# A hybrid Gated-DeltaNet and window-attention layer: the value head moved forward, inverses held back, small copies on ScalarE, two projections once over their weights

## The chip, the cores and the metric

One core of one Trainium2 chip. The metric is the device time of one execution in microseconds; the kernel before was run three times for it. TensorE does the matrix products, VectorE, ScalarE and GpSimd the rest; the profile names these engines PE (with PEld for its weight loads), DVE, ACT and POOL, and SP is the queue that issues most transfers.

## The reference, cut to what matters

The input is x of 2048 tokens by 1024 channels, float32. One projection w_in gives the inputs of two token mixers; their outputs are gated, merged, projected by w_out, added to the residual and normalized.

```python
q, k, v = split(silu(causal_conv4(h[..., :1536])))
o_a = chunked_gated_delta_rule(l2norm(q) * 128**-0.5, l2norm(k), v, g, beta)
y_a = o_a * rsqrt(mean(o_a**2) + 1e-6) * dn_norm_w * silu(dn_z)
q_b, k_b = partial_rope(sw_q), partial_rope(sw_k)
y_b = banded_sink_attention(q_b, k_b, v_b, sinks) * silu(sw_z)
merged = sigmoid(gate_a) * (y_a @ w_branch[0]) + sigmoid(gate_b) * (y_b @ w_branch[1])
out = merged @ w_out
r = alpha * x + out
y = (r - mean(r)) * rsqrt(var(r) + 1e-5) * ln_g + ln_b
```

The delta rule (four heads of 128) goes over blocks of tokens: a triangular system per block is inverted, and a state S of 128x128 per head is carried from block to block. The window attention has eight query heads of 64 in two groups of four, each with one key head, and looks back 128 tokens.

## The kernel before

**Tiling.** The tokens go in four chunks of T = 512, each of NB = 4 blocks of 128. Every product is float32 in three fast products: both factors are split into a high and a low part, and high x high, high x low and low x high are summed in PSUM (`prods`, L175 to L177). The split weights are made in chunk 0, kept in DRAM, and fetched again for each use in later chunks (tile wb, four buffers, `W_SPLIT`; the DRAM tensors are named kw_ and the weight, kw_o for the output projection).

**The order of TensorE's work** is written by hand. `ORDER` (L45) is a string of pieces for chunks 1 to 3 (`ORDER_FIRST`, L44, for chunk 0): kv, key and value rows of the window; k0 to k3, q0 to q3, v0 to v3, the projections of a head of the delta rule, each with its convolution (`conv_silu`, L309: a copy xs, three steps L318 and the end L321 on VectorE, with a halo of three columns carried from chunk to chunk); p, a quarter of the output projection of the chunk before (`project`, L674); g and z, gates; w0 and w1, the query projections of the window with rope (`window_q`, L541). After the fourth p the layer norm of the chunk before is spawned (`layer_norm`, L703; its rows are L718 and L719).

The class `Order` (L821) interleaves these dense pieces with tasks that have to wait for other engines: after each dense step it advances a planned time and lets a task make its next step if the latency written beside it (the `LAT_` numbers, L40) has passed. `finish(name)` runs the tasks up to that one with no dense work between: it moves the planned time on. The tasks of a head are `front` (decays, L365 for k, L389 for the triangular system), `inverse` (L423: the tile su is fetched by a transfer, a part of it zeroed at L924, and 16 steps L936 and L937 on VectorE solve the diagonal blocks of 32), `levels` (L428 to L472, the larger blocks), L485 (v transposed on TensorE), and `back`, the recurrence over the four blocks: L497 (S times k), bt L499 on VectorE, L502 and L505 on TensorE, wc L504 on VectorE, L508 and L510 on TensorE, S L509 on VectorE. `query_rows` (L560) transposes the roped queries (L565) and `attend` (L574) does the window attention.

**Query projection before.** `window_q` makes two passes, of two token blocks each. The first pass fetches four quarters of the weights and keeps them, the second uses the kept ones. Behind each pass come the ropes of its two blocks (`rope`, L877: a copy kr on ScalarE at L881, four small operations on VectorE at L885 to L887) and a task for their transposes. The second pass is followed by `st.finish("qT0")`. `project` makes two passes over kept quarters in the same way, and adds x at L688 (yBh, yBl).

The order on the other engines follows from a scheduler; each engine executes its list in order. The functions with the line numbers of the profile:

## Time and profile before

| | us |
|---|---|
| median of 3 runs | 1702.67 (1699.82 to 1708.82) |
| profiled execution | 1703.38 |
| its span, first to last instruction | 1701.6 |
| TensorE busy | 1623.3 (95%) |
| VectorE busy | 1019.1 (60%) |
| ScalarE busy | 534.6 (31%) |
| GpSimd busy | 313.1 (18%) |

The span is what the profile shows of the execution; the rest of the execution's time lies around it. The mean granted clock of TensorE is 0.987 of full speed. Matrix products are pipelined, so the busy time of TensorE is not its time at peak. A wait is put down to what came last.

### The profile page before, as it was taken

To read this page: it belongs to the slowest core of one execution; us is meant where nothing else is said; L and a number is where in the kernel's file an instruction comes from. 1 tells how busy PE (TensorE), PEld (TensorE's weight loads), DVE (VectorE), ACT (ScalarE), POOL (GpSimd) and SP (SyncE) were. 2 spreads that over 40 slices of the span, in tenths; PEclk is the share of its full clock that TensorE was granted. 3 is DMA by queue.
4 is the path that set the end of the run, shared out by engine and by line. 5 is a ranking of instruction groups with operands and counts; after the bars stand their busy time and mean duration, and the time that the engine had idled before them with its cause. 6 is when DMAs were issued, how large, how long until landed. Compare 5 with 4: busy or idle time off the path is not lost.

```text
span 1701.6 us, 27308 instructions
## 1 busy us (share of the span) xinstructions
PE 1623.3 (95%) x9846; PEld 1365.4 (80%) x9846; DVE 1019.1 (60%) x3202; ACT 534.6 (31%) x1484; POOL 313.1 (18%) x318
## 2 busy tenths in 40 slices
PE   8989999989979999999999999999999999999997
PEld 6867878878968778788987877888887887888787
DVE  6687678447577756434548774733556777463155
ACT  3454445424222432331302343323120244232110
POOL 4543544441401111010101111001010111100001
PEclk9999999999999999999999999999999999999999
DMA  8765676657765446457566644646566654564762
GB/s 304 237 228 186 200 256 200 232 194 251 249 240 177 141 127 177 141 161 238 170 213 208 184 138 129 192 137 199 170 195 212 201 159 119 149 190 143 272 207 77
DMA packets 189159, 323.39 MB, mean 190 GB/s; under 512 B 31072, under 2 KB 45408, under 8 KB 188896
## 3 DMA queue, kind: packets, MB, share of 16 engines
q1 hardware_dynamic: 185184, 316.40, 58.5%
q0 software_dynamic: 3840, 5.25, 1.5%
q8 instruction: 78, 1.28, 0.3%
q14 instruction: 57, 0.47, 0.1%
HBM read 244.97 MB, written 71.37 MB: 186 GB/s over the span
## 4 chain that ended last, share of the span: by engine, by line
PE 80%; DVE 9%; DMA 7%; ACT 1%; issue 1%; SPq 1%; POOL 1%; ACTq 0%; DVEq 0%; POOLq 0%
PE mm L175 22%; PE mm L177 21%; PE mm L176 21%; DMA wb<-kw_o 2%; PE pp L630 2%; PE pp L622 2%; DVE xt L936 1%; PE pp L591 1%; DVE xi L937 1%; PE pd L508 1%; PE pp L592 1%; PE pd L502 1%; DMA s<-in_lnp 1%; DVE k L318 1%; PE pd L510 1%
## 5 line engine op out<-in xcount | busy, mean ns | idle before, releaser
L175 PE MATMUL mm<-xh,wb 128*128 128x512 f32 x1128 | 472.0, 418 | 3.1 <-DVE mv L692 1.6
L177 PE MATMUL mm<-xh,wb 128*128 128x512 f32 x1128 | 447.4, 397 | 0.0
L176 PE MATMUL mm<-xl,wb 128*128 128x512 f32 x1128 | 445.8, 395 | 0.0
L177 PEld LDWEIGHTS mm<-xh,wb 128*128 128x128 f32 x1128 | 213.1, 189 | 50.3
L175 PEld LDWEIGHTS mm<-xh,wb 128*128 128x128 f32 x1128 | 214.1, 190 | 47.2 <-issue 4.5
L176 PEld LDWEIGHTS mm<-xl,wb 128*128 128x128 f32 x1128 | 215.0, 191 | 37.4
L157 POOL TENSOR_TENSOR wb<-w,wb 128x512 fp32r<-128x512 f32 (+1 forms) x110 | 146.3, 1332 | 182.2 <-ACT wb L156 167.8
L175 PE MATMUL mm<-wb,s 128*128 128x256 f32 x384 | 111.8, 291 | 10.3 <-DMA wb<-kw_o 6.3
L175 PE MATMUL mm<-wb,xh 128*128 128x256 f32 (+1 forms) x384 | 114.0, 297 | 6.6 <-DVE ba L264 3.2
L176 PE MATMUL mm<-wb,xh 128*128 128x256 f32 (+1 forms) x384 | 108.5, 282 | 0.3 <-POOL wb L157 0.3
L176 PE MATMUL mm<-wb,s 128*128 128x256 f32 x384 | 108.5, 283 | 0.0
L177 PE MATMUL mm<-wb,s 128*128 128x256 f32 x384 | 108.5, 283 | 0.0
L177 PE MATMUL mm<-wb,xl 128*128 128x256 f32 (+1 forms) x384 | 108.1, 281 | 0.0
L156 ACT ACTIVATE wb<-w 128x512 fp32r<-128x512 f32 (+1 forms) x110 | 68.9, 628 | 106.9 <-PE mm L177 54.6
L936 DVE TENSOR_TENSOR xt<-su,xi 128x16 f32<-128x16 f32 (+15 forms) x256 | 88.4, 345 | 5.7
L175 PEld LDWEIGHTS mm<-wb,s 128*128 128x128 f32 x384 | 73.1, 190 | 14.6 <-DMA wb<-kw_o 8.2
L608 ACT ACTIVATE s<-s,nm 128x256 f32<-128x256 f32 (+1 forms) x128 | 62.6, 491 | 68.4 <-DVE nm L602 68.4
L175 PEld LDWEIGHTS mm<-wb,xh 128*128 128x128 f32 x384 | 72.5, 189 | 10.0 <-issue 6.2
L937 DVE TENSOR_REDUCE xi<-xt 128x8 f32<-128x16 f32 (+15 forms) x256 | 74.7, 292 | 6.2
L176 PEld LDWEIGHTS mm<-wb,s 128*128 128x128 f32 x384 | 73.1, 190 | 0.2
L177 PEld LDWEIGHTS mm<-wb,s 128*128 128x128 f32 x384 | 73.0, 190 | 0.0
L176 PEld LDWEIGHTS mm<-wb,xh 128*128 128x128 f32 x384 | 72.4, 189 | 0.7 <-POOL wb L157 0.6
(664 smaller groups left out, 3104.5 us busy)
## 6 DMA issues: line engine op xcount, KB each, us to landing
wb<-kw_h SPq DMA_DIRECT2D x96, 512.0 KB, 4.1
wb<-kw_g SPq DMA_DIRECT2D x96, 512.0 KB, 4.0
w<-in_wg SPq DMA_DIRECT2D x106, 256.0 KB, 4.1
wb<-kw_b SPq DMA_DIRECT2D x48, 512.0 KB, 4.2
wb<-kw_o SPq DMA_DIRECT2D x36, 512.0 KB, 5.0
kw_h<-wb SPq DMA_DIRECT2D x32, 512.0 KB, 3.6
kw_g<-wb SPq DMA_DIRECT2D x32, 512.0 KB, 3.5
wb<-kw_q SPq DMA_DIRECT2D x24, 512.0 KB, 3.9
```

What stands on the lines that cost most here:

```text
L156: nc.scalar.activation(hi, raw, AF.Copy)
L157: nc.gpsimd.tensor_tensor(lo, raw, hi.bitcast(F32), ALU.subtract)
L175: nc.tensor.matmul(ps, sh, mh, start=(first and i == 0), stop=False)
L176: nc.tensor.matmul(ps, sh, ml, start=False, stop=False)
L177: nc.tensor.matmul(ps, sl, mh, start=False, stop=(last and i == n))
L318: nc.vector.scalar_tensor_tensor(r, xs[:, s:s + T], convw[:, n, s:s + 1], r, ALU.mult, ALU.add)
L502: nc.tensor.matmul(ps, q_[:, b], bt, start=True, stop=True)
L608: nc.scalar.activation(s[:, g, k0:], s[:, g, k0:], AF.Exp, bias=nm[:, g:g + 1], scale=0.125, accum_out=su[:, g:g + 1])
L622: nc.tensor.transpose(psp[:, kb, g], ss[v][:, g, P * kb:P * kb + P], ident)
L630: nc.tensor.matmul(psY[64 * v:64 * v + 64], c.vs[b + kb][:, 64 * v:64 * v + 64], pTs[v][:, kb], start=(kb == kbs[0]), stop=(kb == 1))
L936: nc.vector.tensor_tensor(tx[:, :, :, :n], u, x, ALU.mult)
L937: nc.vector.tensor_reduce(xi[:, :, i:i + 2], tx[:, :, :, :n], AX.X, ALU.add)
```

## The change

Four parts. (1) In `ORDER`, v0 stands after the first p instead of behind k1. (2) The latency LAT_M from `front` to `inverse` is 10000 instead of 4400 ns in the planner's time, the memset of su moves from `small_inverse` into `inverse`, placed behind the last VectorE instruction issued so far, and the planned time of an inverse step is 300 + 35n instead of 420 + 40n ns. (3) The two copies of the halo in `conv_silu` (L314, L319; 96 in all) go from VectorE to ScalarE. (4) A new helper `prod_all` takes each quarter of the weights once for all four token blocks, in the order 0, 2, 1, 3; the four sums are open in two PSUM banks of two blocks each. `project` and `window_q` use it. In `window_q` the ropes of all four blocks then follow the whole product. Lines of the changed kernel stand 10 to 13 further down (L502 becomes L515, L497 L510, L508 L521, L499 L512, L504 L517, L565 L577, L485 L498, L718 L728, L688 L698).

```diff
--- before.py
+++ after.py
@@ -37,12 +37,12 @@
 
 PE_R, PE_F, PE_T, PE_Q = 216, 218, 109, 45
 
-LAT_INV, LAT_B, LAT_S, LAT_N, LAT_SM, LAT_D, LAT_M, LAT_K, LAT_Q, LAT_Y, LAT_F, LAT_W = 29600, 2700, 2300, 7700, 9200, 5400, 4400, 1400, 7900, 8300, 4100, 2300
+LAT_INV, LAT_B, LAT_S, LAT_N, LAT_SM, LAT_D, LAT_M, LAT_K, LAT_Q, LAT_Y, LAT_F, LAT_W = 29600, 2700, 2300, 7700, 9200, 5400, 10000, 1400, 7900, 8300, 4100, 2300
 FIRST = ("h01", "h00", "h02")
 
 
 ORDER_FIRST = "start g kv w0 g k1 g g q1 g g g z0 v1 g z1 k2 q2 v2 w1 k3 g q3 g v3 g g g g z2 z3 g g"
-ORDER = "kv k0 q0 p p p p k1 v0 q1 g w0 v1 z0 k2 q2 v2 g g g k3 z1 g q3 g w1 v3 g g g g z2 g g g z3 g g g"
+ORDER = "kv k0 q0 p v0 p p p k1 q1 g w0 v1 z0 k2 q2 v2 g g g k3 z1 g q3 g w1 v3 g g g g z2 g g g z3 g g g"
 
 P_ALOG, P_DTB, P_DNW, P_SINK, P_CONV = 0, 4, 8, 9, 17
 P_N = 17 + 48
@@ -167,14 +167,15 @@
                 for i in range(2):
                     yield half_w(name, i, 2)
 
-        def prods(ps, terms, first=True, last=True):
+        def prods(ps, terms, first=True, last=True, shared=False):
+
 
             n = len(terms) - 1
             cost = PE_R * ps.free_size() / 512
             for i, (sh, sl, mh, ml) in enumerate(terms):
-                nc.tensor.matmul(ps, sh, mh, start=(first and i == 0), stop=False)
-                nc.tensor.matmul(ps, sh, ml, start=False, stop=False)
-                nc.tensor.matmul(ps, sl, mh, start=False, stop=(last and i == n))
+                nc.tensor.matmul(ps, sh, mh, start=(first and i == 0), stop=False, skip_group_check=shared)
+                nc.tensor.matmul(ps, sh, ml, start=False, stop=False, skip_group_check=shared)
+                nc.tensor.matmul(ps, sl, mh, start=False, stop=(last and i == n), skip_group_check=shared)
                 if cost * 3 * (i % 2 + 1) > 1000 or i == n:
                     yield cost * 3 * (i % 2 + 1)
 
@@ -197,6 +198,15 @@
                 for ps, b in zip(pss, blocks):
                     yield from prods(ps, [(tok(ah[2 * g + k], b), tok(al[2 * g + k], b), wh[:, k], wl[:, k])
                                           for k in range(2)], g == 0, g == 3)
+
+        def prod_all(pss, ah, al, ww, load=None):
+
+            for g, (wh, wl) in enumerate(ww):
+                if load:
+                    load(2 * g + 1)
+                for b in (0, 2, 1, 3):
+                    yield from prods(pss[b // 2][:, b % 2], [(tok(ah[2 * g + k], b), tok(al[2 * g + k], b), wh[:, k], wl[:, k])
+                                                             for k in range(2)], g == 0 and not b % 2, g == 3, True)
 
         def kept(ww, into):
             for w in ww:
@@ -311,12 +321,12 @@
             n = j * 4 + h
             xs = ph.tile([P, T + 3], F32, name="xs")
             nc.scalar.activation(xs[:, 3:], ps, AF.Copy)
-            nc.vector.tensor_copy(xs[:, :3], halo[:, n])
+            nc.scalar.activation(xs[:, :3], halo[:, n], AF.Copy)
             r = ph.tile([P, T], F32, name="qkv"[j], bufs=(1, 2, 1)[j])
             nc.scalar.activation(r, xs[:, 3:], AF.Copy, scale=convw[:, n, 3:4])
             for s in range(3):
                 nc.vector.scalar_tensor_tensor(r, xs[:, s:s + T], convw[:, n, s:s + 1], r, ALU.mult, ALU.add)
-            nc.vector.tensor_copy(halo[:, n], xs[:, T:])
+            nc.scalar.activation(halo[:, n], xs[:, T:], AF.Copy)
             nc.scalar.activation(xs[:, :T], r, AF.Tanh, scale=0.5)
             nc.vector.scalar_tensor_tensor(r, xs[:, :T], 1.0, r, ALU.add, ALU.mult)
             c.qkv[j, h] = r.rearrange("p (b t) -> p b t", b=NB)
@@ -421,6 +431,9 @@
             yield 4 * PE_F, 0
 
         def inverse(h, su, xi):
+
+            with tc.issue_after(next(i for i in reversed(nc.cur_bb.bb.instructions) if i.engine == mybir.EngineType.DVE)):
+                nc.vector.memset(view(su, 33, [[66, 16]]), 0.0)
             yield from small_inverse(tc, pt.tile([P, 256], F32, name="xt"), su, xi.rearrange("p (c i) -> p c i", i=32))
             nc.sync.dma_start(out=at(scr_p[h % 2], 0, [[P, P], [1, P]]), in_=xi)
             yield None, 0
@@ -543,15 +556,14 @@
             if gp:
                 st.finish("window0")
             c.qT = [pa.tile([P, NB, 2, P], F32R, name=n, bufs=1) for n in ("qT0", "qT1")]
-            ww, more = [], quarters([f"q{gp}{i}" for i in range(2)])
+            pss = [mm.tile([P, 2, 256], F32, name="mm") for _ in range(2)]
+            yield from prod_all(pss, c.xh, c.xl, quarters([f"q{gp}{i}" for i in range(2)]), lambda k: load_x(c, k))
             for b0 in (0, 2):
-                pss = [mm.tile([P, T], F32, name="mm")[:, :256] for _ in range(2)]
-                yield from prod_tc(pss, (b0, b0 + 1), c.xh, c.xl, ww if b0 else kept(more, ww), lambda k: load_x(c, k))
                 if b0:
                     st.finish("qT0")
                 qr = [pa.tile([P, 256], F32, name="kr") for _ in range(2)]
-                for b, ps in enumerate(pss):
-                    rope(nc, sm, qr[b], ps, 4, cos[:, c.i * NB + b0 + b], sin[:, c.i * NB + b0 + b])
+                for b in range(2):
+                    rope(nc, sm, qr[b], pss[b0 // 2][:, b], 4, cos[:, c.i * NB + b0 + b], sin[:, c.i * NB + b0 + b])
                 st.spawn(f"qT{b0}", query_rows(c, b0, qr), LAT_Q)
             for g in range(2):
                 yield from silu2(c, f"zb{2 * gp + g}")
@@ -675,15 +687,13 @@
 
             if not eg:
                 c.ra = [py.tile([P, 2, D], F32, name=n) for n in ("yBh", "yBl")]
-            ww, more = [], quarters([f"o{eg}{i}" for i in range(2)])
             es = slice(256 * eg, 256 * eg + 256)
             xr, pss = [], [mm.tile([P, 2, 256], F32, name="mm") for _ in range(2)]
             for bp in range(2):
                 xr.append(pa.tile([P, 2, 256], F32, name="s"))
                 t0 = c.i * T + bp * 256
                 nc.sync.dma_start(out=xr[bp], in_=xn[t0:t0 + 256, es].rearrange("(b p) e -> p b e", p=P))
-            for b2 in range(2):
-                yield from prod_tc([ps[:, b2] for ps in pss], (b2, 2 + b2), c.mh, c.ml, ww if b2 else kept(more, ww))
+            yield from prod_all(pss, c.mh, c.ml, quarters([f"o{eg}{i}" for i in range(2)]))
             for bp in range(2):
                 nc.vector.scalar_tensor_tensor(c.ra[bp][:, :, es], xr[bp], 2.0 * ALPHA, pss[bp], ALU.mult, ALU.add)
 
@@ -921,7 +931,6 @@
     rows = su.rearrange("p (m r k) -> p m r k", r=2, k=32)
     tm = t.rearrange("p (m k) -> p m k", k=32)
     nc = tc.nc
-    tc.keep_in_program_order(nc.vector.memset(view(su, 33, [[66, 16]]), 0.0))
     for m in range(0, 16, 8):
         ms = slice(m, m + 8)
         nc.vector.tensor_tensor(tm, rows[:, ms, 1], view(su, 66 * m + 1, [[66, 8], [0, 32]]), ALU.mult)
@@ -935,7 +944,7 @@
         x = view(xi, i, [[32, 4], [0, 2], [1, n]])
         nc.vector.tensor_tensor(tx[:, :, :, :n], u, x, ALU.mult)
         nc.vector.tensor_reduce(xi[:, :, i:i + 2], tx[:, :, :, :n], AX.X, ALU.add)
-        yield None, 420 + 40 * n
+        yield None, 300 + 35 * n
 
 
 def tables(seq):
```

TensorE at the end of the query projection w0 of chunk 1, before. L508 and L510 belong to the recurrence of a head (wc, S and bt are its tiles on VectorE), L565 to the transposes of the queries, mm<-wb is the query projection, mm<-xh the next product:

```order
L175 MATMUL mm<-wb,xh 128x256
L176 MATMUL mm<-wb,xh 128x256
L177 MATMUL mm<-wb,xl 128x256
L175 MATMUL mm<-wb,xh 128x256
L176 MATMUL mm<-wb,xh 128x256
L177 MATMUL mm<-wb,xl 128x256
L508 MATMUL pd<-wc,ktl 128x128
L510 MATMUL pd<-wc,dt 128x128
L565 MATMUL pp<-ct,kr 128x128 x4
L175 MATMUL mm<-xh,wb 128x512
```

The same place in the changed kernel:

```order
L176 MATMUL mm<-wb,xh 128x256
L177 MATMUL mm<-wb,xh 128x256
L178 MATMUL mm<-wb,xl 128x256
L515 MATMUL pd<-bt,q__4891 128x128
L518 MATMUL pd<-S,qd 128x128
L521 MATMUL pd<-wc,ktl 128x128
L523 MATMUL pd<-wc,dt 128x128
L510 MATMUL pd<-S,k 128x128
L577 MATMUL pp<-ct,kr 128x128 x4
L515 MATMUL pd<-bt,q__4891 128x128
L518 MATMUL pd<-S,qd 128x128
L176 MATMUL mm<-xh,wb 128x512
```

Before, twelve matmuls of the projection lie between the pair L502, L505 and the pair L508, L510, and one pair and the transposes between the projection's last matmul and the next product. In the changed kernel seven of the recurrence's products and the transposes stand there in one row. The same is seen at all six query projections of chunks 1 to 3, and in a similar form at the two of chunk 0.

VectorE around the convolution of v0 in chunk 1, before. L318 and L321 are its steps, L718 and L719 rows of the layer norm of chunk 0, with mv, rs and s its factors:

```order
L318 SCALAR_TENSOR_TENSOR v<-xs,par,v 128x512
L718 SCALAR_TENSOR_TENSOR yBh<-yBh,mv,s 128x256
L718 SCALAR_TENSOR_TENSOR yBl<-yBl,mv,s 128x256 x2
L719 SCALAR_TENSOR_TENSOR yBh<-yBh,rs,s 128x256
L718 SCALAR_TENSOR_TENSOR yBh<-yBh,mv,s 128x256 x2
L718 SCALAR_TENSOR_TENSOR yBl<-yBl,mv,s 128x256 x2
L318 SCALAR_TENSOR_TENSOR v<-xs,par,v 128x512
L719 SCALAR_TENSOR_TENSOR yBh<-yBh,rs,s 128x256
L719 SCALAR_TENSOR_TENSOR yBl<-yBl,rs,s 128x256 x2
L719 SCALAR_TENSOR_TENSOR yBh<-yBh,rs,s 128x256 x2
L719 SCALAR_TENSOR_TENSOR yBl<-yBl,rs,s 128x256 x2
L321 SCALAR_TENSOR_TENSOR v<-xs,v 128x512
```

The same steps in the changed kernel; L698 takes the sums of the output projection, the memset, L936 and L937 belong to the inverse:

```order
L698 SCALAR_TENSOR_TENSOR yBh<-s,mm 128x2x256
L698 SCALAR_TENSOR_TENSOR yBl<-s,mm 128x2x256
L402 SCALAR_TENSOR_TENSOR m_4790<-pd,nci,dt 128x128 x4
L530 TENSOR_SCALAR qsum<-qsum 128x4
L328 SCALAR_TENSOR_TENSOR v<-xs,par,v 128x512 x2
L426 TENSOR_TENSOR dt<-pd,dt 128x512
L328 SCALAR_TENSOR_TENSOR v<-xs,par,v 128x512
L436 MEMSET su 128x16
L936 TENSOR_TENSOR xt<-su 128x256
L937 TENSOR_TENSOR su<-su,xt 128x8x32
L331 SCALAR_TENSOR_TENSOR v<-xs,v 128x512
```

Before, fifteen rows of layer norm lie among these steps of v0. In the changed kernel they are gone from there, and the memset of su stands between the third step of v0 and its last, behind the two rows of L698.

VectorE during the first step of the recurrence in w0 of chunk 1, in the changed kernel (bt is L512, wc L517; L728 and L729 are the layer norm, L331 the last step of the convolution of q1):

```order
L512 SCALAR_TENSOR_TENSOR bt<-pd,neG,vt 128x128
L728 SCALAR_TENSOR_TENSOR yBl<-yBl,mv,s 128x256
L331 SCALAR_TENSOR_TENSOR q<-xs,q 128x512
L728 SCALAR_TENSOR_TENSOR yBh<-yBh,mv,s 128x256 x2
L728 SCALAR_TENSOR_TENSOR yBl<-yBl,mv,s 128x256
L384 TENSOR_SCALAR nci<-cc 128x4
L728 SCALAR_TENSOR_TENSOR yBl<-yBl,mv,s 128x256
L729 SCALAR_TENSOR_TENSOR yBh<-yBh,rs,s 128x256 x2
L729 SCALAR_TENSOR_TENSOR yBl<-yBl,rs,s 128x256 x2
L517 TENSOR_SCALAR wc<-pd,cc 128x128
```

Nine rows of layer norm stand between bt and wc. And at the end of the same projection (S is L522; L895 to L897 are the rope, L522 needs L521 on TensorE):

```order
L522 SCALAR_TENSOR_TENSOR S<-S,eGl,pd 128x128
L512 SCALAR_TENSOR_TENSOR bt<-pd,neG,vt 128x128
L426 TENSOR_TENSOR dt<-pd,dt 128x512
L895 TENSOR_TENSOR rope<-mm,ct 128x64 x2
L896 TENSOR_TENSOR kr<-rope 128x4x8
L897 TENSOR_TENSOR kr<-rope 128x4x8
L517 TENSOR_SCALAR wc<-pd,cc 128x128
L895 TENSOR_TENSOR rope<-mm,ct 128x64 x2
L896 TENSOR_TENSOR kr<-rope 128x4x8
L897 TENSOR_TENSOR kr<-rope 128x4x8
L522 SCALAR_TENSOR_TENSOR S<-S,eGl,pd 128x128
L512 SCALAR_TENSOR_TENSOR bt<-pd,neG,vt 128x128
```

One rope stands ahead of wc, a second between wc and S.

## Rows read from the trace of the kernel before

**Rows 1.** Page, part 1: busy us, share of the span, instructions of each engine.

```profile
PE 1623.3 (95%) x9846; PEld 1365.4 (80%) x9846; DVE 1019.1 (60%) x3202; ACT 534.6 (31%) x1484; POOL 313.1 (18%) x318
```

**Rows 2.** Waits of PE: line waiting, releaser, us in total, times, longest us.

```profile
PE pd L485 <- DVE v L321: 14.2, 3, 7.2
...
PE mm L175 <- DMA wb<-kw_o: 6.3, 10, 1.5
...
PE pd L502 <- DVE bt L499: 5.8, 4, 1.6
...
PE mm L175 <- DVE yBh L688: 3.9, 2, 3.4
...
PE pp L622 <- DVE osum L518: 2.6, 3, 0.9
...
PE pd L508 <- DVE wc L504: 2.0, 5, 0.6
```

**Rows 3.** Windows: start and end, length, busy us of each engine, PEclk, DMA share, GB/s.

```profile
504.00:507.70 3.70, 3.70 (x12) 3.01 (x13) 2.74 (x6) 1.24 (x2) 0.00 (x0) 0.50 1.03 421
917.40:920.70 3.30, 3.30 (x11) 2.61 (x10) 3.30 (x10) 0.81 (x4) 0.00 (x0) 0.50 0.02 5
1331.30:1337.10 5.80, 5.80 (x18) 4.82 (x19) 5.80 (x16) 2.44 (x9) 0.00 (x0) 0.50 0.01 3
449.70:453.10 3.40, 3.40 (x19) 3.40 (x17) 3.03 (x11) 0.00 (x0) 1.16 (x1) 0.50 0.93 283
606.00:610.00 4.00, 2.25 (x13) 1.88 (x14) 3.96 (x23) 2.56 (x13) 0.53 (x1) 1.00 0.40 129
```

**Rows 4.** Timeline: start, length, engine, line, operation, tiles, idle before it and releaser.

```profile
446.88 0.07 DVE L924 MEMSET su<- 128x16 f32 x1 [5.95 <-DMA su<-scrm]
...
480.49 0.60 ACT L313 ACTIVATE xs<-mm 128x512 f32<-128x512 f32 x1 [2.77 <-PE mm L177]
...
489.21 0.68 DVE L321 SCALAR_TENSOR_TENSOR k<-xs,k 128x512 f32<-128x512 f32 x1
...
503.14 0.69 DVE L321 SCALAR_TENSOR_TENSOR v<-xs,v 128x512 f32<-128x512 f32 x1
```

**Rows 5.** Timeline of PE and DVE at the end of head 0's recurrence, chunk 1.

```profile
604.76 0.28 PE L592 MATMUL pp<-kTl,qT 128*128 128x256 f32 x1
...
604.88 0.28 PE L591 MATMUL pp<-kT,qT 128*128 128x256 f32 x1
...
606.96 0.35 DVE L499 SCALAR_TENSOR_TENSOR bt<-pd,neG,vt 128x128 f32<-128x128 f32 x1
...
607.36 0.49 PE L502 MATMUL pd<-bt,q__5767 128*128 128x128 f32 x2 [1.62 <-DVE bt L499]
...
608.46 0.49 PE L508 MATMUL pd<-wc,ktl 128*128 128x128 f32 x2 [0.39 <-DVE wc L504]
```

**Rows 6.** Waits of DVE, columns as in the waits of PE.

```profile
DVE halo L319 <- ACT xs L313: 32.7, 18, 7.4
...
DVE su L924 <- DMA su<-scrm: 24.7, 14, 5.9
...
DVE yBh L718 <- DMA s<-in_lnp: 8.1, 3, 3.2
```

**Rows 7.** Groups by line: count, busy us and mean ns, idle before and releaser.

```profile
L314 DVE COPY xs<-halo 128x3 f32<-128x3 f32 x48 | 14.7, 306 | 0.8
...
L319 DVE COPY halo<-xs 128x3 f32<-128x3 f32 x48 | 9.3, 194 | 33.1 <-ACT xs L313 32.7
...
L605 ACT ACTIVATE es<-es 128x2 f32<-128x2 f32 x64 | 10.5, 188 | 0.0
...
L885 DVE TENSOR_TENSOR rope<-mm,ct 128x64 f32<-128x64 f32 x64 | 11.5, 218 | 5.5 <-ACT kr L881 4.6
...
L886 DVE TENSOR_TENSOR kr<-rope 128x32 f32<-128x32 f32 x32 | 6.4, 200 | 0.6
...
L718 DVE SCALAR_TENSOR_TENSOR yBh<-yBh,mv,s 128x256 f32<-128x256 f32 x24 | 10.7, 479 | 8.1 <-DMA s<-in_lnp 8.1
```

## The prediction

> **What bounds the kernel now.** I first read the page: TensorE is busy 95% of the span, VectorE 60%, ScalarE 31% [rows 1]. The work of TensorE is the same in both kernels (the change adds and drops no matmul), so time can only come from the places where TensorE stands, and from the time after them at half clock. The second view is therefore TensorE's waits [rows 2]: the largest row is 14.2 us in three waits of L485 (the transposes of v) for the v convolution, then 6.3 us for weight quarters of the output projection (kw_o), 5.8 us for bt and 2.0 us for wc (the recurrence of head 1), 3.9 us for yBh and 2.6 us for osum. The third view asks what the clock does after a stall [rows 3]. Behind the three v waits the granted clock is 0.50 (the 1.2 GHz level) for 3.70, 3.30 and 5.80 us of busy TensorE, and behind the 3.4 us wait for yBh for 3.40 us. In the stretch 606 to 610 us TensorE stands 1.75 of 4 us in pieces, and the clock stays at 1.00 (2.4 GHz); two stretches like it, at 1018 and 1434 us, read 1.00 too. So here one long stall cost half of what followed it, and several short ones did not.
>
> **The sum, part by part.** The profiled execution took 1703.38 us, span 1701.6; the median of the runs is 1702.67, 0.71 less. About 0.5% (8.5 us) is what a measurement of this kernel can tell from no change.
>
> *v forward.* The last step of v0's convolution started at 503.14 and freed L485 [rows 4]. It is late because layer-norm rows of the chunk before stand between its steps on VectorE (the order of VectorE at v0). Now v0's product follows the first projection, the convolution ends on VectorE before layer norm starts, and three projections lie between it and L485: 3 x 96 matmuls of 128x256, which start 0.12 us apart [rows 5], some 34 us against a longest wait of 7.2. Gain: 14.2, plus half of 3.70 + 3.30 + 5.80 us at half clock = 6.4. Together **20.6**. What else v0's product covered: k1's convolution, whose copy began at 480.49 and whose last step began at 489.21, so 9.4 us with its 0.68 [rows 4]. Between k1's product and its first reader the order leaves dense work for about 11 us (from the same spacing), so I cost that at nothing; cover gone, it would be at most a few us per chunk.
>
> *Inverses held.* At 446.88 VectorE reached the memset of su after 5.95 us behind su's transfer [rows 4]; yBh's two rows of the projection stood behind it, and TensorE waited for them. VectorE waits there 24.7 us in 14 waits [rows 6]. The change plans 10.0 instead of 4.4 us from front to inverse, so the memset comes when the transfer has landed, and v0's steps and yBh pass ahead of it. Gain: 3.9 us of waits [rows 2] and half of 3.40 = 1.7 at half clock: **5.6**. The inverse starts 5.6 us later by the plan, but its 16 steps are planned at 300 + 35n instead of 420 + 40n (n = 2 to 32), 14.3 instead of 17.6 us, so its end moves by only 2.3 us.
>
> *Projection once over its weights.* In the first pass of before each quarter served 12 matmuls, 1.4 us; all four buffers were then held through a second pass. Now a quarter serves 24 (2.9 us) and is free at once. Ten waits for kw_o, 6.3 us [rows 2], none over 1.5 us: a transfer then has twice the time. Taken: **6.3** (at the least 3, if half of the waits are starts of a projection).
>
> *The old place without cover.* At k2, finish("back0") ran head 0's last recurrence step with nothing dense in it: 1.62 us for bt at 607.36, 0.39 for wc at 608.46 [rows 5], and 0.9 for osum [rows 2], at three chunks. In the new order the step ends earlier and lies between products. Gain 3 x (1.62 + 0.39 + 0.87) = **8.6**. All gains: 20.6 + 5.6 + 6.3 + 8.6 = **41.1 us**.
>
> *Query projection once over its weights.* This is the loss. Before, the first pass's ropes and transposes fell under the second pass. Now all ropes follow the last product, and finish("qT0") follows at once: its planned 7.9 us run off with no product between, so the recurrence steps that are due run bare (the order of TensorE at that place): L515, L518, L521, L523, L510, L577 x4, L515, L518. Each link of that chain goes through VectorE; from L502 at 607.36 to L508 at 608.46 it is 1.10 us [rows 5]. Three links (L515 over wc to L521, over S to L510, over bt to the next L515), then that L515 and L518, 0.22 each: 3.74 us. TensorE's own work in them: seven such products (two instructions of 0.11, which I estimate from the spacing of 0.12 in the same rows) and four transposes of 0.11: 1.98. So 1.76 us stand at least, per place; there are eight (two per chunk). On VectorE the first rope stands ahead of wc; a rope is two operations of 0.22 us and two of 0.20 [rows 7], 0.84, and half of it may overlap. I take 1.76 + 0.44 = **2.2 us**, 8 x 2.2 = **17.6**. Upper end: all four ropes ahead (3.4 us) and half clock behind (1.7): 6.8. The lower end is 1.5, for chunk 0, whose ends hold fewer steps.
>
> A rule speaks against this row by row reading. Rows 3 say that short stalls in a 4 us stretch leave the clock at 1.00. The Trainium skill (TensorE: Matmul & The Clock Gate, "A second HAM failure mode: psum-queue depth-cycling") says that micro-idling between groups of matmuls can throttle the clock again although no gap looks long. By the rows the sum keeps 17.6; by that rule it would be higher, and that is rival 3.
>
> *Layer norm between bt and wc.* With v0 gone from its place, nine layer-norm rows of 0.48 us [rows 7], a q step and small ones stand between bt and wc of the first recurrence step in each w0 (VectorE's new order): about 5.2 us, with 0.35 for wc. From L510 (0.5) over bt (0.35) to L521 that makes some 6.4 us, and the order gives TensorE about 6.5 us of work. Break-even; I take 1 us in each of three chunks, **3**, between 0 and 12 (a 3 us wait for layer norm's transfer ahead of it [rows 6]).
>
> *Copies on ScalarE.* 96 copies leave VectorE (14.7 + 9.3 us and 32.7 us of waits for xs at their head [rows 6, 7]). On ScalarE a 128x2 operation takes 0.188 us [rows 7], so 18 us on an engine busy 31%. Between 0 and 4 us of gain; VectorE's relief is used up by the terms above. Taken: 0. The cover is the dense products behind each convolution; gone, 0.4 us per convolution.
>
> Sum: 1703.38 - 41.1 + 17.6 + 3 = 1682.9, so **1683 us**.
>
> **The rivals.**
>
> 1. *The ends become the bound (slower).* At each of the eight ends all four ropes stand ahead of wc and S on VectorE, so 1.76 + 3.4 us, and the half clock follows, 1.7: 6.8 us, 55 in all. 1703.38 - 41.1 + 3 + 55 = **1720 us**. For it: the order puts two ropes inside the chain, and stalls over 3.4 us were followed by 0.50 [rows 3]. Against: only one rope stands ahead of the first wc, and block 0's product ends early enough to rope before. From 4.8 us per end (38.1 of 41.1 - 3) nothing is gained, and from 5.8 (46.6) the kernel is slower by 0.5%. Chance 0.11.
>
> 2. *The wait of v moves to bt.* Layer norm waits for its own transfer for 8.1 us in three waits [rows 6]; that wait, and its rows, now stand ahead of bt and wc. Then three places cost 3 us and half clock behind (1.7) instead of 1: 14 us instead of 3, **1694 us**. For it: VectorE's new order. Against: one wait in a chunk, of the four loads that the code makes there. Chance 0.13.
>
> 3. *The clock oscillates.* Each of the eight ends is followed by a half-clock stretch like 449.70 to 453.10 [rows 3], 1.7 us: 13.6 us, **1697 us**. For it: stalls of 2 us are between the 1.6 that left the clock up and the 3.4 that did not [rows 2, 3]; the page named above gives the rule. Against: 606 to 610 at 1.00. Chance 0.10.
>
> 4. *Chunk 0 waits for its inverses.* The hold of 5.6 us delays four inverses that feed each other's levels, where no projection covers. If two of them come through, 11 us: **1694 us**. Against: the end moves by 2.3 us only. Chance 0.10.
>
> 5. *The copies and freed quarters give more than I count*, and the ends cost 1.8 each: **1670 us**. Chance 0.07. That the change does not do what it says I exclude: the order shows each move.
>
> **How the numbers follow.** The forecast has 0.49, with a range of its own of 1674 to 1693 (ends of 1.5 to 3.2 us, kw_o of 3 to 6.3, layer norm 0 to 8). The likeliest is 1683. The whole range, 8 in 10: from 1670, the fifth, to 1700, which takes in rivals 2 to 4 and leaves out the slow one and the tails. Faster by over 0.5% means below 1694.2: nearly all of the forecast (0.46), the fifth (0.07), and half of rivals 2 and 4 (0.12) with a little of 3: 0.67. Slower means above 1711.2: rival 1 and mixtures of two rivals: 0.11. The rest, 0.22, is within 0.5%.
>
> **What would show it.** Right: no wait for v of L498 (the old L485) over 1 us, and clock 1.00 at the start of each chunk's heads; yBh and kw_o together under 4 us; bt and wc together risen from 7.8 to some 18 us, in waits of 1 to 2 us at the eight ends of the query projections, with the clock at 1.00 there. Wrong: waits of 3 us and more for wc, S or kr at these ends, or 0.50 behind them (rivals 1, 3); L515 or L521 waiting under layer-norm rows (rival 2); waits of chunk 0 for xi or p_ (rival 4).

## The result and the profile after

The changed kernel takes 1770.57 us (median of 4 runs, 1767.73 to 1771.53), the kernel before, measured beside it, 1701.24: ratio 1.0398, 95% interval 1.0375 to 1.0421. It is slower by about 4%, where a gain of 1% was forecast. The profiled execution took 1767.73 us with a span of 1766.0, 64.4 us more than before.

The page's busy times, answering to [rows 1]:

```profile
PE 1648.9 (93%) x9846; PEld 1386.4 (79%) x9846; DVE 1008.6 (57%) x3106; ACT 546.4 (31%) x1580; POOL 313.4 (18%) x318
```

TensorE executes the same 9846 instructions in 25.6 us more of busy time, and stands 117.1 us (1766.0 - 1648.9) instead of 78.3: of the 64.4 us, 38.8 are standing and 25.6 are busy time. The granted clock is 0.968 on the mean, before 0.987. In the traces TensorE is busy at 0.50 for 83.9 us, before for 32.1; half of the difference is 25.9, so the half clock accounts for the longer busy time.

TensorE's waits, answering to [rows 2] (waiting line, releaser, us in total, times, longest):

```profile
PE pd L419 <- DVE wc L517: 7.4, 3, 2.5
...
PE pd L521 <- ACT junk L421: 5.0, 3, 1.7
...
PE pd L463 <- DMA p__5959<-scrp: 4.8, 1, 4.8
...
PE pd L463 <- DMA p__6808<-scrp: 4.5, 1, 4.5
...
PE mm L176 <- DVE yBh L698: 4.3, 2, 4.0
PE pd L521 <- DVE wc L517: 4.3, 7, 2.9
...
PE pd L515 <- DVE bt L512: 0.9, 2, 0.5
```

The rows for v (14.2 us) and for kw_o (6.3 us) are gone and bt nearly so, as forecast. The row for yBh stayed: 4.3 after 3.9. New are 26 rows of L463, the first products of the levels, which wait for p_, the inverse read back from DRAM: 55.2 us in all, 10 of them over 2 us; 14.1 us of the 55.2 are in chunk 0. In the trace before the same line (L450) has one row of 0.4 us. New are also the first two rows, L419 for wc and L521 for ScalarE's reading of L419's product, 12.4 us. Waits for wc at L521 rose from 2.0 to 4.3. The prediction had named as signs bt and wc risen to some 18 us (0.9 + 4.3 are seen) and yBh and kw_o together under 4 (4.3).

Windows, answering to [rows 3]; first the end of the query projection w0 in chunk 1, then three stretches behind waits of L463, then one behind the waits of L419 and L521 in chunk 1, and one behind the end of w0 in chunk 2:

```profile
533.00:537.00 4.00, 3.54 (x24) 2.83 (x24) 3.04 (x16) 1.47 (x5) 0.00 (x0) 1.00 0.99 254
562.50:566.50 4.00, 3.45 (x22) 2.77 (x23) 1.76 (x4) 0.90 (x2) 0.00 (x0) 0.50 0.14 27
642.00:646.00 4.00, 3.02 (x24) 2.58 (x25) 2.26 (x6) 0.57 (x2) 0.00 (x0) 0.53 0.15 31
1077.00:1081.00 4.00, 3.42 (x24) 2.91 (x25) 2.26 (x6) 0.90 (x2) 0.00 (x0) 0.50 0.15 25
522.70:529.60 6.90, 5.25 (x24) 4.84 (x25) 3.02 (x10) 1.47 (x8) 0.00 (x0) 0.51 0.60 225
969.90:973.30 3.40, 3.40 (x11) 2.82 (x11) 3.30 (x17) 1.41 (x4) 0.62 (x1) 0.50 0.10 24
```

At seven of the eight ends the clock is 1.00; behind the one in chunk 2, which stands 4.5 us, it is 0.50. Behind each of the ten L463 waits of over 2 us comes a stretch at 0.50; TensorE is busy in these ten for 50.6 us, of which half, 25, is the price of the clock.

The chain at the end of w0 in chunk 1, in the timeline of TensorE:

```profile
533.19 0.39 PE L515 MATMUL pd<-bt,q__4891 128*128 128x128 f32 x2
...
534.03 0.49 PE L521 MATMUL pd<-wc,ktl 128*128 128x128 f32 x2 [0.23 <-DVE wc L517]
...
534.97 0.49 PE L510 MATMUL pd<-S,k 128*128 128x128 f32 x2 [0.22 <-DVE S L522]
...
535.29 0.60 PE L577 MATMUL pp<-ct,kr 128*128 128x128 f32 x4
...
535.90 0.49 PE L515 MATMUL pd<-bt,q__4891 128*128 128x128 f32 x2
```

From 533.19 over the steps that the prediction listed it runs to 536.4, where the next product begins. That is 3.2 us with 1.98 of work: 1.2 us of standing, less than the forecast 2.2. Measured in the same way (time from the first of these steps to the next product, less the work in it at 0.11 us each) seven of the eight ends in this trace stand 1.1 to 1.5 us and one 4.5, all together 13.0 (forecast 17.6). So in this kernel the place that the prediction watched cost less than forecast, and the loss lies elsewhere.

Where it lies is seen by following one head (the third of chunk 1) from its triangular system to its levels. Before:

```profile
582.71 1.16 PE L389 MATMUL pd<-k 128*128 128x128 f32 x8
...
594.34 0.07 DVE L924 MEMSET su<- 128x16 f32 x1 [0.62 <-DMA su<-scrm]
...
611.34 0.41 DVE L937 TENSOR_REDUCE xi<-xt 128x8 f32<-128x256 f32 x1
...
617.62 0.21 PE L450 MATMUL pd<-p__6761,m 32*32 32x32 f32 x1
```

The memset comes 11.6 us behind the products L389, the last step of the inverse begins 17.0 us behind it and ends at 611.75, and L450 follows at 617.62 without a wait. After:

```profile
599.90 1.16 PE L399 MATMUL pd<-k 128*128 128x128 f32 x8
...
617.51 0.07 DVE L436 MEMSET su<- 128x16 f32 x1
...
638.38 0.42 DVE L946 TENSOR_REDUCE xi<-xt 128x8 f32<-128x256 f32 x1
...
640.48 1.73 SPq L451 DMA_DIRECT2D p__6808<-scrp  x4
...
642.07 0.24 PE L463 MATMUL pd<-p__6808,m 32*32 32x32 f32 x2 [4.51 <-DMA p__6808<-scrp]
```

The memset now comes 17.6 us behind L399, 6.0 later. The last step of the inverse begins 20.9 us behind it instead of 17.0, the read of p_ is issued at 640.48, and L463 has waited 4.51 us for it. This is one of the heads with a long delay: over all 16 heads the memset comes 15.7 instead of 12.4 us behind the triangular system, and the last step begins 20.2 instead of 19.0 us behind the memset, 4.5 us later in all.

TensorE was there as early as the planner had put it. By the code, `levels` waits for two things in planned time: LAT_INV = 29.6 us behind the triangular system, and the planned end of the inverse. Before, that end lies 29.2 us behind the triangular system (3.6 to the spawn, 4.4 for LAT_M, 3.6 for two first steps, 17.6 for the sixteen), in the changed kernel 31.5 (3.6 + 10.0 + 3.6 + 14.3). So the planner puts the reader some 2 us later, and the machine's inverse ends 4.5 us later on the mean and 9.9 in this head.

### The profile page after: what moved, and what is told of

It is laid out like the page before. It is cut to its first block, busy times and chain, and to the rows that moved or that the text cites. A ratio compares the mean times of both kernels' runs of the same rounds, so it can differ in the third digit from the quotient of the medians.

```text
span 1766.0 us, 27224 instructions
## 1 busy us (share of the span) xinstructions
PE 1648.9 (93%) x9846; PEld 1386.4 (79%) x9846; DVE 1008.6 (57%) x3106; ACT 546.4 (31%) x1580; POOL 313.4 (18%) x318
## 3 DMA queue, kind: packets, MB, share of 16 engines
q0 software_dynamic: 3840, 5.25, 1.3%
## 4 chain that ended last, share of the span: by engine, by line
PE 71%; DVE 14%; DMA 9%; ACT 2%; issue 1%; SPq 1%; POOL 1%; ACTq 0%; DVEq 0%; POOLq 0%
PE mm L176 20%; PE mm L178 19%; PE mm L177 19%; DMA scrp<-xi 2%; DMA s<-in_lnp 2%; DVE xt L945 2%; PE pp L642 2%; PE pp L634 2%; DVE xi L946 1%; DMA su<-scrm 1%; PE pd L515 1%; PE pd L510 1%; DVE k L328 1%; DVE yBh L728 1%; DMA xl<-kw_o 1%
## 5 line engine op out<-in xcount | busy, mean ns | idle before, releaser
L176 PE MATMUL mm<-xh,wb 128*128 128x512 f32 x1128 | 477.8, 424 | 0.6 <-DMA wb<-kw_h 0.6
L178 PE MATMUL mm<-xh,wb 128*128 128x512 f32 x1128 | 452.2, 401 | 0.0
L177 PE MATMUL mm<-xl,wb 128*128 128x512 f32 x1128 | 451.8, 400 | 0.0
L176 PEld LDWEIGHTS mm<-xh,wb 128*128 128x128 f32 x1128 | 218.0, 193 | 51.6 <-issue 10.1
L178 PEld LDWEIGHTS mm<-xh,wb 128*128 128x128 f32 x1128 | 216.7, 192 | 51.8
L177 PEld LDWEIGHTS mm<-xl,wb 128*128 128x128 f32 x1128 | 218.7, 194 | 38.7
L176 PE MATMUL mm<-wb,xh 128*128 128x256 f32 (+1 forms) x384 | 116.3, 303 | 6.1 <-DMA wb<-kw_kv 2.9
L177 PE MATMUL mm<-wb,xh 128*128 128x256 f32 (+1 forms) x384 | 110.5, 288 | 0.5 <-POOL wb L157 0.5
L176 PEld LDWEIGHTS mm<-wb,xh 128*128 128x128 f32 x384 | 74.9, 195 | 9.4 <-issue 6.6
L176 PEld LDWEIGHTS mm<-wb,s 128*128 128x128 f32 x384 | 73.8, 192 | 5.8 <-DVE yBh L698 4.8
L177 PEld LDWEIGHTS mm<-wb,xh 128*128 128x128 f32 x384 | 74.7, 195 | 0.9 <-POOL wb L157 0.7
L178 PEld LDWEIGHTS mm<-wb,xl 128*128 128x128 f32 x384 | 74.5, 194 | 0.0
L177 PEld LDWEIGHTS mm<-wb,s 128*128 128x128 f32 x384 | 73.6, 192 | 0.3
```

The costliest lines, as they stand in the source:

```text
L176: nc.tensor.matmul(ps, sh, mh, start=(first and i == 0), stop=False, skip_group_check=shared)
L177: nc.tensor.matmul(ps, sh, ml, start=False, stop=False, skip_group_check=shared)
L178: nc.tensor.matmul(ps, sl, mh, start=False, stop=(last and i == n), skip_group_check=shared)
```

## The experiments

All ratios are to the kernel before, measured beside each run; the changed kernel's is 1.0398.

**1. Which half of the hold.** Kernel e1 undoes the second part of the change (the hold), e2 only the planned steps, e3 only LAT_M; e4 makes the second part alone on the kernel before.

```diff
-... 5400, 10000, 1400, ...
+... 5400, 4400, 1400, ...
-        yield None, 300 + 35 * n
+        yield None, 420 + 40 * n
```

The first pair of lines is e3, the second e2, both and the memset back in `small_inverse` e1; e4 has them the other way round on the kernel before.

> The changed kernel with its second part undone (LAT_M 4400, memset of su in small_inverse, steps at 420 + 40n). Theory H, the hold makes the inverses late for the levels: the 60 us of waits of L463 (the first products of the levels) for p_ fall to under 5, the some 20 us of half clock behind them go too, time 1690 us (1680 to 1700). Rival R, the moved v0, layer norm and bare recurrence steps delay the inverse on VectorE: over 30 us of waits of L463 stay, time over 1735.

1745.8 us, 1.0244 (1.0223 to 1.0266): rival R's number, not H's.

> The changed kernel with the planned inverse steps at 420 + 40n again, LAT_M still 10000 and the memset still in inverse. H with the late start as the cause: the plan for the levels moves by about 1 us only, waits of L463 between 40 and 65 us, time 1750 to 1772. If instead the shorter plan of the steps is the cause: waits under 15 us, time about 1700.

1736.43 us, 1.0187 (1.0166 to 1.0208), waits for p_ of 19.8 us instead of 55.2: between the two expectations.

> The changed kernel with LAT_M 4400 alone put back. H with the late start as the cause: waits of L463 under 10 us, time 1685 to 1702. If the shorter plan of the steps is the cause: waits over 40 us, time over 1740. Rival R: the same, over 1735.

1748.75 us, 1.0257 (1.0221 to 1.0293), waits 34.7 us. With LAT_M at 4400 the plan of the steps makes no difference that can be told: e3 lies at e1. With LAT_M at 10000 it does: e2 alone takes 34 us off the changed kernel, more than e1 (25) and e3 (22). By the code the old steps move the planned end of the inverse, and with it the reader, some 3.5 us later, where the expectation of e2 had counted 1.

> The kernel before with the second part alone. H: the levels (L450 there plus 3 lines) wait some 50 to 65 us for p_, and the half clock behind adds 15 to 25; less 5 us gained at yBh: 1765 to 1785. R: waits under 10 us, 1695 to 1705.

1727.3 us, 1.0122 (1.009 to 1.0154), waits for p_ of 20.5 us, among them (TensorE's waits of e4; L453 is the levels' line there):

```profile
PE pd L453 <- DMA p__2790<-scrp: 8.7, 1, 8.7
...
PE pd L453 <- DMA p__1910<-scrp: 4.1, 1, 4.1
...
PE pd L453 <- DMA p__10965<-scrp: 1.9, 1, 1.9
```

So the hold by itself loses about 21 us, where the prediction counted a gain of 5.6, and it is a real part of the L463 waits. The first two of these rows are two heads of chunk 0 (L453 at 173.8 and 257.7 us), which with a short second wait each make 14.0 of the 20.5 us; the wait for yBh is gone in e4. But theory H was too large: without the hold 34.5 us of the waits of the changed kernel stay (TensorE's waits of e1; L460 is the levels, L507 waits for S, L399 is the triangular system):

```profile
PE pd L399 <- DVE wc L514: 9.7, 3, 3.3
...
PE pd L507 <- DVE S L519: 8.1, 9, 2.4
...
PE pd L460 <- DMA p__14347<-scrp: 6.3, 1, 6.3
```

Something else makes the levels early or the inverses late.

**2. Each other part alone.** On the kernel before: v0 moved (e7), prod_all in both projections (e8), the copies (e12). Each is the part of the change as shown in its diff. And the changed kernel with the levels planned later (e13):

```diff
-LAT_INV, LAT_B, ... = 29600, 2700, ...
+LAT_INV, LAT_B, ... = 35200, 2700, ...
```

> The kernel before with v0 behind the first projection and nothing else. By the prediction's term, v forward gains 20 us: about 1683. Theory L, layer norm takes v0's place: the waits of L485 for v go (14 us and their half clock), but layer-norm rows now delay wc and the memset of su of the next inverse in each w0, and the levels behind it wait for p_ some 6 us in three chunks: 1700 to 1720, with waits of the levels (L450) over 12 us.

1715.51 us, 1.0072 (1.0049 to 1.0095). TensorE's waits of e7:

```profile
PE mm L175 <- DMA wb<-kw_o: 11.5, 9, 3.1
PE pd L502 <- DVE bt L499: 5.8, 4, 1.6
PE pd L389 <- DVE yBh L719: 5.7, 2, 3.2
...
PE pd L450 <- DMA p__14423<-scrp: 3.1, 1, 3.1
```

The wait for v is gone, and with it should go 20 us; instead the kernel is slower by some 11. TensorE waits 11.5 us instead of 6.3 for weights of the projection, 5.7 for layer-norm rows (L719) ahead of the triangular system, and 7.6 instead of 0.4 at the levels, and its busy time is 5.5 us longer (1628.8). These add up to 23.6 more, against the 14.2 that went. The row for bt stays as it was. Theory L has the time right and the waits of the levels too high (over 12 expected).

> The kernel before with prod_all in both projections and nothing else (v0, the hold and the copies as before). By the prediction's terms: 6.3 and 8.6 gained, 17.6 lost, 1705 (1697 to 1715). If the projections are what the rest of the loss comes from: over 1725.

1759.22 us, 1.0326 (1.0276 to 1.0376): this part carries most of the loss.

> The kernel before with the 96 small copies on ScalarE and nothing else; TensorE's order is the same. By the prediction: 0 to 4 us gained, 1699 to 1705. If ScalarE's copies hold up the convolutions or the exponentials: over 1710.

1704.99 us, 1.0000 (0.9983 to 1.0018): the copies cost and gain nothing, as forecast.

> The changed kernel with LAT_INV 35200 instead of 29600: the levels are planned 5.6 us later, as much as the inverse is held. Theory H: waits of the levels (L463) for p_ fall from 60 to under 12 us, with their half clock 50 to 70 us are gained, 1700 to 1720. If the inverses come late for another reason (VectorE stands behind recurrence rows that TensorE reaches late): waits over 30 us stay, over 1735.

1734.14 us, 1.0183 (1.0158 to 1.0208), waits for p_ 29.0 us. Planning the levels 5.6 us later by LAT_INV, as much as the inverse is held, recovers some 36 us of the change's loss, where H had claimed 50 to 70. Like e2, it moves the reader later in the plan.

**3. Which projection, and its finish.** e14: prod_all in `project` alone; e15: in `window_q` alone; e17: as e15, one gate product between the first two ropes and finish("qT0"); e19: the whole change without the hold, with that later finish. The edit of the last two:

```diff
                 if b0:
+                    yield from silu2(c, f"zb{2 * gp}")
                     st.finish("qT0")
...
-            for g in range(2):
-                yield from silu2(c, f"zb{2 * gp + g}")
+            yield from silu2(c, f"zb{2 * gp + 1}")
```

> The kernel before with prod_all in the output projection alone. Theory J (the loss sits where window_q calls finish(qT0) with no product behind it): TensorE's plan is the one of before, the waits for kw_o (6 to 8 us) go, 1695 to 1704. If using each quarter once for four blocks is itself slower: over 1715.

1693.71 us, 0.9928 (0.9905 to 0.9951): faster by 0.7%. The page's busy times of e14, and the first rows of TensorE's waits:

```profile
PE 1620.7 (96%) x9846; PEld 1366.5 (81%) x9846; DVE 1015.8 (60%) x3202; ACT 535.8 (32%) x1484; POOL 314.6 (19%) x318
```

```profile
PE pd L512 <- DVE bt L509: 10.1, 6, 2.3
PE mm L176 <- DVE yBh L696: 7.8, 3, 4.6
PE pd L495 <- DVE v L331: 6.4, 3, 3.5
```

The rows for kw_o are gone, and the wait for v is 6.4 instead of 14.2 us; those for bt and yBh have grown. This one part is the fastest kernel that was run, and faster than both kernels of the change.

> The kernel before with prod_all in the query projection alone. J: the planner's time jumps by 6.8 us at each of eight finish(qT0) instead of 0.3; TensorE pays it there in waits for wc, S and bt, or later, when the levels come before their inverses; with the half clock the whole loss of both projections, 1745 to 1765. If the output projection carries the loss: under 1715.

1772.01 us, 1.0391 (1.0361 to 1.0422): the query projection alone costs as much as the whole change. TensorE's waits of e15:

```profile
PE pd L507 <- DVE S L519: 13.5, 7, 3.0
...
PE pd L512 <- DVE bt L509: 8.1, 8, 4.2
...
PE pd L460 <- DMA p__2663<-scrp: 4.8, 1, 4.8
```

The bare ends stand 31 us in this kernel, the levels wait 25.1.

> The query projection alone as in the run before it, but with one gate product (zb) between the first two ropes and finish(qT0), so that the jump is 1.8 us per end. J: most of the loss goes, 1700 to 1718; no wait of 2 us or more at the eight ends. If the ropes behind the product are themselves the cost (VectorE busy with four in a row): over 1735.

1747.42 us, 1.0255 (1.0236 to 1.0273). By the number the rival's, but the run does not tell: the edit puts the second pair of transposes right ahead of the attention, and TensorE stands before L600 at eight places, mostly 2.6 to 2.8 us and once 5.9, some 25 us in all. That wait is the experiment's own; the profile names no releaser for most of it, so that it comes from the transposes is not shown.

> The changed kernel without the hold and with the late finish: v forward, copies on ScalarE, both projections once over their weights. J with theory L (layer norm delays the next inverse): the gain of v is given back at the levels, 1695 to 1720. If the parts other than hold and finish gain what the prediction said: 1670 to 1690.

1732.1 us, 1.0156 (1.0136 to 1.0177), with the same wait before L600 in it, so over every expected range.

**4. The planner's jump by itself.** What finish() does is move the planned time to the next due step until its task is done. I added up these jumps, in planned time, from the code's own numbers: at finish("qT0") 0.3 us per call in chunks 1 to 3 before (3.7 us over all eight), 6.8 per call in the changed kernel (54.1 over all eight). e20 takes the finish out of e15, with a tile of another tag for the last two ropes; e21 takes it out of the whole change; e22 has both projections once over their weights, no finish, the copies, and v0 and inverses as before; e26 is e22 with LAT_W 6300 instead of 2300; e23 is the change without the hold and with the query projection of before. The edit of e20:

```diff
                 if b0:
-                    st.finish("qT0")
-                qr = [pa.tile([P, 256], F32, name="kr") for _ in range(2)]
+                    pair = pa.tile([P, 2, 256], F32, name="s")
+                    qr = [pair[:, b] for b in range(2)]
+                else:
+                    qr = [pa.tile([P, 256], F32, name="kr") for _ in range(2)]
```

And e28 leaves the kernel before as it is and only moves the planner's time:

```diff
                     st.finish("qT0")
+                    end = st.now + 6500
+                    while st.now < end:
+                        st.run()
+                        st.now = min([end] + [t[0] for t in st.tasks if t[0] > st.now])
```

> The kernel before (two passes, ropes as before), with the planner's time moved on by 6.5 us behind each finish(qT0), tasks that come due run there, nothing else. J: 25 to 50 us lost by this alone, 1730 to 1755, in waits for S, bt and wc at the eight ends and for p_ at the levels behind them. Rival (the ropes in a row, not the jump): under 1715.

1760.45 us, 1.0321 (1.0284 to 1.0358), above the expected range. No product, rope or transfer was changed, only the order in which tasks follow. TensorE's waits of e28 (L497 for S, L502 for bt, L457 behind the levels):

```profile
PE pd L497 <- DVE S L509: 13.4, 7, 3.8
...
PE pd L502 <- DVE bt L499: 7.9, 8, 2.7
...
PE mm L175 <- DMA wb<-kw_o: 5.8, 9, 1.1
...
PE pd L457 <- DVE q__11408 L443: 2.7, 1, 2.7
```

The ends stand 28 us here, the levels wait 12, and the half clock adds 31 of busy time (1654.5 against 1623.3 us). With the projection as before, the jump alone makes a loss of the size of e15's: that the jump by itself is enough for it (theory J) is shown, for this one size of jump.

> The query projection alone once over its weights, with no finish(qT0): the ropes of blocks 2 and 3 go to a tile of another tag, and both transposes follow 7.9 us later under the gate products. The planner's total time is that of before. J: 1698 to 1710, no waits of 2 us behind the eight projections, waits of the levels (L463 minus 3) under 6 us. Rival (four ropes in a row): over 1735.

1731.28 us, 1.015 (1.0116 to 1.0183), between J and its rival. Without the finish 41 of e15's 66 us go, the wait for S (13.5 us in e15) is gone, and the levels wait 1.7 us. What stays is another wait (TensorE's waits of e20; L602 is the attention's first product):

```profile
PE pp L602 <- DMA qT<-pT: 14.0, 7, 3.4
...
PE pd L512 <- DVE bt L509: 8.3, 7, 1.9
...
PE pp L602 <- DVE xi L948: 5.3, 2, 3.3
```

> The changed kernel without that finish. J with theory H: the 60 us of the query projection go, the hold's loss of 20 to 25 and v forward's 10 stay, the output projection's gain of 11 stays: 1715 to 1735. Rival: over 1755.

1759.91 us, 1.0317 (1.0283 to 1.035): only about 11 us better than the change. With the hold in, the levels still wait 47.9 us for p_. The two causes overlap: undone alone, the hold gives back 25 us (e1) and the finish 11.

> Both projections once over their weights, no finish(qT0), copies on ScalarE; v0 and the inverses as before. J: the gain of the output projection alone (1693.7) stands: 1688 to 1699. Rival: over 1725.

1717.35 us, 1.0071 (1.0047 to 1.0095): the attention waits for qT as in e20; the expected range is missed.

> The kernel of e22 (both projections once over their weights, no finish, copies on ScalarE; 1717) with LAT_W 6300 instead of 2300, so that the attention is planned 4 us later. If the waits for qT (19 us) are only that the attention comes too early: they fall under 5 us and the time to 1692 to 1702. If the four ropes and transfers in a row are the cost, they move: waits of VectorE and TensorE elsewhere, over 1710.

1700.1 us, 0.9963 (0.9949 to 0.9977). TensorE's waits of e26:

```profile
PE pd L495 <- DVE v L331: 13.7, 3, 4.8
...
PE pp L602 <- DVE yb L646: 2.7, 2, 2.4
```

No wait for the transposed queries is left. The four ropes in a row are thus not what costs; the attention had been planned for queries whose first half was roped half a projection earlier. But e26 does not beat e14: the query projection once over its weights brings nothing, since no wait for its weights was there to be gained.

> v forward, the output projection once over its weights and the copies on ScalarE; query projection and inverses as before. If the two edits add up: 1715.5 + 1693.7 - 1704.6, about 1705. If the waits for kw_o that v forward alone raised from 8 to 13 us go as well: 1692 to 1700.

1707.36 us, 1.0014 (0.9997 to 1.0032). v forward takes back the gain of the output projection, nearly as by adding up. With the hold and the query projection both undone, all but 0.14% of the loss of 3.98% is gone: these two parts carry it.

## Why the prediction was wrong, step by step

**v forward (20.6 gained).** The wait of L485 went, all 14.2 us. The step that failed is the cover at the old place, which the prediction put at nothing, at most a few us per chunk. It looked at k1's convolution alone and not at layer norm, VectorE work of some 15 us per chunk (32 rows of 0.48) that v0's product had covered too. In e7 23.6 us of other waits and busy time came for the 14.2, 5.7 of them behind layer-norm rows by name. Alone the move loses (1.0072).

**Inverses held (5.6 gained).** The step "its end moves by only 2.3 us" failed: it is a difference of planned durations. From the memset to the last step the new plan counts 16.5 us and the old one counted 19.5; measured on the mean it is 20.2 and was 19.0. So the change cut the plan of the steps below what VectorE takes, while the reader follows the plan. Between the last step and L450 in the head shown lay 5.9 us before; the round trip through DRAM takes 3.3 (after: 638.80 to 642.07), so the slack was about 2.6, a number that the trace before held and the prediction did not read. e2 and e13, which move the reader later in the plan, take off 34 and 36 us. Alone the hold loses 1.2%, although there the wait for yBh is gone as forecast; in the changed kernel it stayed, 4.3 us. Rival 4 had the right mechanism and, for chunk 0, about the size: 11 us forecast at 0.10, 14.0 measured in e4 and 14.1 in the changed kernel. The other 41 us of L463's waits lie in chunks 1 to 3, where it saw none.

**Projection once over its weights (6.3 gained).** Right: kw_o's waits are gone. Alone the part gains 0.7%, about 12 us, twice the term; the wait for v, which fell by 7.8 us in e14, was no part of it.

**The old place without cover (8.6 gained).** In the changed kernel bt waits 0.9 us instead of 5.8 and the row for osum is gone. But not by the step that the prediction gave, v0's new place: with that alone (e7) bt waits 5.8 us as before. What removed it was not separated.

**Query projection (17.6 lost).** The ends stand 13.0 us in the changed kernel, near the term, but that is luck: with the query projection alone (e15) they stand 31, with the jump alone (e28) 28. The step that failed is the price of the jump. The prediction wrote that the planned 7.9 us of finish("qT0") "run off with no product between" and then priced only the steps in that gap. It did not follow what becomes of the planned time. By the code the planner counts 8.8 us for such an end (6.8 of jump, 2.0 of work), and TensorE spent 3.2 at the end shown: every step planned from there comes some 5.6 us early for inverses whose steps VectorE has yet to do. In e15 the levels then wait 25.1 us with no hold in the kernel. e28 shows that the jump alone costs 3.2%.

**Layer norm between bt and wc (3 lost).** The mechanism was right, the size not. The timeline of VectorE and TensorE in w0 of chunk 1:

```profile
516.71 0.34 DVE L512 SCALAR_TENSOR_TENSOR bt<-pd,neG,vt 128x128 f32<-128x128 f32 x1
...
517.97 1.91 DVE L728 SCALAR_TENSOR_TENSOR yBh<-yBh,mv,s 128x256 f32<-128x256 f32 x2
...
521.46 0.87 DVE L729 SCALAR_TENSOR_TENSOR yBl<-yBl,rs,s 128x256 f32<-128x256 f32 x2
...
522.25 0.34 DVE L517 TENSOR_SCALAR wc<-pd,cc 128x128 f32<-128x128 f32 x1
...
522.64 1.07 PE L419 MATMUL pd<-ct,q 128*128 128x128 f32 x4 [2.50 <-DVE wc L517]
...
525.37 0.79 PE L521 MATMUL pd<-wc,ktl 128*128 128x128 f32 x2 [1.66 <-ACT junk L421]
```

wc begins 5.5 us behind bt, near the 5.2 worked out, though one pair of layer-norm rows took 1.91 us where another took 0.87. By the releasers named, L419 stood 2.50 us until wc had read its product, and L521 another 1.66 until ScalarE had read L419's. So the work counted as cover could not run past these two. Three chunks: 7.4 + 5.0 = 12.4, over the upper bound of 12, and the clock behind is 0.51 for 5.25 us of busy TensorE (522.70 to 529.60), which loses 2.6 more there and some 7 in the three chunks.

**Copies (0).** Right: ratio 1.0000.

**The rivals.** Rival 3 (the rule of the Trainium skill, TensorE: Matmul & The Clock Gate, "A second HAM failure mode: psum-queue depth-cycling") is not seen at seven of the eight ends: the clock at 533 to 537 us is 1.00. Behind the one that stands 4.5 us it is 0.50. The half clock came behind long waits, as in [rows 3], only at other lines. Rival 2's place was right, and its 14 us were too few: 12.4 of waits and some 7 of half clock. Rival 1 did not happen in the changed kernel; the ends came nearer to its eight times 5.2 us of standing with the query projection alone (31).

The parts alone multiply to 1.0072 x 1.0122 x 0.9928 x 1.0391 x 1.0000 = 1.0517, the change measured 1.0398: the losses do not add up, as e1, e21 and e23 show too. How the rest of e13's waits (29.0 us) splits between hold and jump was not separated further.

## What to carry to other kernels

In a kernel whose order comes from planned latencies, a change can be right at the place it edits and lose behind it: read for every moved producer when its reader is planned, and from the trace the slack between them, before pricing the move. A planned duration is a number to hold against the trace: here the steps of an inverse were planned at 16.5 us that had taken 19.0 on the mean. A wait of the planner that is run with no work behind it is not a small bubble: it sets the plan ahead of the machine, and in e28 that cost 28 us of standing at the place, 12 at the levels behind it and 31 of half clock. Make parts alone: here half of one part of four (the output projection once over its weights, 0.9928) was worth keeping.

## What was not expected of the hardware

That the same matmuls cost so much more busy time: 25.6 us of the 64.4 are not waits but slower products, most of them behind waits of 2.5 to 5 us, at a granted clock of 0.50 to 0.53 in the rows above. In the three windows behind L463 TensorE is busy for 3.0 to 3.5 of 4 us at that clock, so 1.5 to 1.7 us are lost in each beside the wait itself.
